# Low halves of 96 weight units by accumulating DMAs in a two-layer decoder trunk

## The chip, the cores and the metric

The kernel runs on one core of one Trainium2 chip. The metric is the device time of one execution in microseconds (us), lower is better. A profile gives, beside the time, the span from the first to the last instruction of the program on the core. The engines are TensorE (PE, with its weight loads PEld), VectorE (DVE), ScalarE (ACT), GpSimd (POOL) and SyncE (SP), which here issues every DMA.

## The reference

Two layers over a sequence of 512 positions with 1024 channels, all float32. Layer 0 mixes tokens with a gated DeltaNet, layer 1 with a Conformer convolution module; each layer then cross-attends into a fixed memory of 256 positions and applies a squared-ReLU MLP.

```python
for layer in range(DEPTH):                      # DEPTH = 2
    if layer % 2 == 0:
        h = h + gated_deltanet(rms_norm(h, ...), ...)
    else:
        h = h + conformer_conv(rms_norm(h, ...), w_pw1, ..., w_pw2, ...)
    h = h + memory_cross_attention(rms_norm(h, ...), rms_norm(mem, ...), w_q, w_kv, w_o)
    h = h + sq_relu_mlp(rms_norm(h, ...), w_up, w_down)
return rms_norm(h, final_norm)

def conformer_conv(h, w_pw1, b_pw1, w_dw, b_dw, ln_g, ln_b, w_pw2, b_pw2):
    u = h @ w_pw1 + b_pw1                       # 1024 -> 2048
    u = u[..., :D_MODEL] * jax.nn.sigmoid(u[..., D_MODEL:])
    c = causal_depthwise_conv(u, w_dw) + b_dw   # width 31
    c = jax.nn.silu(layer_norm(c, ln_g, ln_b))
    return c @ w_pw2 + b_pw2

def sq_relu_mlp(h, w_up, w_down):
    return jnp.square(jax.nn.relu(h @ w_up)) @ w_down   # 1024 -> 4096 -> 1024
```

## The kernel before

Every large product is made with three matmuls in the 32-bit format fp32r. An operand x is split into a rounded half xh and a rest xl = x - xh; a product is then xh·wh + xl·wh + xh·wl (`mm3`, lines 294 to 296; for K/V values and z lines 325 to 327; for the down projection lines 1104 to 1106). The activations are split where they are made, the weights while they stream through.

Weights come in units of 128 x 1024 floats (512 KB), 304 in all, in the order of the list `order`, which is written out by hand: projections of the DeltaNet, K and V of layer 0, output projection, attention and MLP of layer 0, then pw1 of the conformer with K and V of layer 1 behind it (`CONV_SEQ`), pw2, attention and MLP of layer 1. The MLP runs in four groups; a group is eight up units and fourteen down units. The down units are combined from quarters of the down weights on DVE first.

A unit passes through three steps.

- **Load.** `wload` (lines 206 to 217) has SP load the unit into a tile `raw`. The list `loads` gives the order and, for each load, the unit at which it falls due; an ordinary unit's load falls due four units ahead. `raw` has 3 buffers.
- **Split.** `wsplit` (lines 257 to 280) has ACT cast `raw` to the rounded half `wh` (line 273), and then DVE or POOL subtract: `wl = raw - wh` (line 273 calls the helper at line 75). POOL does this for the pw1 units that are not in `PW_DVE` (12 units) and for the first halves of K and V of layer 1 (8 units); DVE does it for all the others. `wh` and `wl` have 3 buffers each. Of the up and down units every fourth uses the tag `ex` instead (4 buffers, shared with some down loads).
- **Use.** `wnext` (lines 281 to 290) hands a unit to the matmuls. Before that it writes the splits of the next units: up to `NW_DN` = 4 counting its own in the MLP, `NW` = 3 elsewhere. A split can start only when the matmuls of an earlier unit have given its buffers free.

A unit for 512 columns is 24 matmuls of 512 columns; a down unit is 12. K and V work for 256 memory positions: a K unit is 24 matmuls of 256 columns, a V unit 12 of 512.

The waits between engines, and the final order on each engine's queue, are made by the framework out of the program order and the data each instruction touches; an engine's queue is then in order. In the conformer stage DVE and POOL also do the depthwise convolution: channel block 0 on POOL with multiplications on ACT (`pool_conv`, lines 1275 to 1290), blocks 1 to 4 on DVE in a PSUM tile (`dve_conv`, 1291 to 1307; line 1298 is its first tap on ACT, line 1304 its copy out), blocks 5 to 7 on PE (line 1335). The layer norm follows on DVE, its results are transposed on PE (line 1366), scaled on ACT (line 1368), and pw2 begins.

POOL's queue also has the sums of squares of the norms in the attention stages, the products of the attention probabilities with their reciprocal sums, and memsets.

Of the kernel before, what the change touches and what calls it, by code (L numbers as in the profile page):

```python
# [8 lines left out]
F32 = mybir.dt.float32  # L9
F32R = mybir.dt.float32r  # L10
AF = mybir.ActivationFunctionType
ALU = mybir.AluOpType
# [26 lines left out]
def tile_trunk(ctx, tc, xT, memT, prm_d, adt_d, bdw_d, tap_d, fin_d, w_ab, w_kq, w_v, w_z, w_dno, w_pw1, w_pw2,  # L39
               w_q, w_k, w_vv, w_o, w_up, w_dn, yT):  # L40
    nc = tc.nc
    pe, act, dve, pool = nc.tensor, nc.scalar, nc.vector, nc.gpsimd
# [3 lines left out]
    up = ctx.enter_context(tc.tile_pool(name="up", bufs=NSLOT))  # L46
# [12 lines left out]
    def big(s, tag, dt=F32):  # L59
        return wp.tile([P, 1024], dt, tag=tag, name=nm(s), bufs=NBIG[tag])  # L60
# [13 lines left out]
    def tt(e, o, a, b, op):  # L74
        return e.tensor_tensor(out=o, in0=a, in1=b, op=op)  # L75
# [65 lines left out]
    pool.memset(eps_ln, LN_EPS)  # L141


    order, loads = [], []

    def plan(key, src, n=2):
        for hf in range(n):
            unit(key, hf, src)

    def unit(key, hf, src):  # L150
        u = len(order)
        order.append((key, hf))
        loads.append((u - NRAW - 1, u, src[:, hf * 1024:(hf + 1) * 1024]))

    def plan_kv(layer, lo=0, hi=8):
        for i in range(lo, hi):
            if i < 4:
                plan(("K", layer, i), w_k[layer, i])
            else:
                plan(("V", layer, i - 4), w_vv[layer, i - 4])  # L160
# [20 lines left out]
    for kind, gq in DN_ORDER:  # L181
        for i in range(2):
            j = gq * 2 + i
# [7 lines left out]
    for kind, i in CONV_SEQ:  # L191
        if kind == "p":
            unit(("pw1", i // 2), i % 2, w_pw1[i // 2])
        elif i < 8:
            unit(("K", 1, i // 2), i % 2, w_k[1, i // 2])
        else:
            unit(("V", 1, i // 2 - 4), i % 2, w_vv[1, i // 2 - 4])
# [6 lines left out]
    ws = {"next": 0, "split": 0, "load": 1, "raw": {0: raw0}, "hl": {}}  # L204
# [14 lines left out]
    def wraw(key):  # L219
        while key not in ws["raw"]:  # L220
            wload()
        return ws["raw"][key]

    def parts(x, two):
        if isinstance(x, list):
            return x
        return [x[:, 0:512], x[:, 512:1024]] if two else [x]

    def dn_raw(layer, g, name, hf):

        def q(n):
            return wraw((layer, g, n, hf))

        def drop(n):
            return ws["raw"].pop((layer, g, n, hf))

        def sub(n, a, b):
            t = [q(k) for k in (n, a, b)]
            for v in zip(*(parts(x, any(isinstance(y, list) for y in t)) for x in t)):
                tt(dve, *v, ALU.subtract)  # L240
            return t[0]

        if name == "M1":
            return q("11"), lambda: sub("11", "12", "11")
        if name == "M5":
            return q("11"), lambda: sub("12", "22", "12")
        if name == "M6":
            return sub("11", "22", "11"), None
        if name == "M3":
            return drop("22"), None  # L250
        if name == "M7":
            return drop("12"), None
        if name == "M2":
            return q("21"), lambda: (sub("11", "21", "11"), drop("21"))
        return drop("11"), None

    def wsplit():
        u = ws["split"]
        ws["split"] += 1
        (kind, i, *j), hf = order[u]  # L260
        then = None
        if kind == "dn":
            raw, then = dn_raw(i, *j, hf)
        else:
            raw = wraw(u)
            del ws["raw"][u]
        extra = kind in ("up", "dn") and u % 4 == 3
        h = big("wh", "ex" if extra else "wh", F32R)
        lo = big("wl", "ex" if extra else "wl", F32R)
        gp = kind == "pw1" and (i, hf) not in PW_DVE or j and kind in "KV" and i == 1 and hf == 0  # L270
        two = isinstance(raw, list)
        for r, h_, l_ in zip(parts(raw, two), parts(h, two), parts(lo, two)):
            ins = [act.copy(h_, r), tt(pool if gp else dve, l_, r, h_.bitcast(F32), ALU.subtract)]  # L273
            if u < 4:
                for x in ins:
                    tc.keep_in_program_order(x)
        if then is not None:
            then()
        ws["hl"][u] = (h, lo)

    def wnext(key, hf):
        i = ws["next"]
        assert order[i] == (key, hf), (order[i], key, hf)
        while ws["load"] < len(loads) and loads[ws["load"]][0] <= i:
            wload()
        nw = NW_DN if key[0] in ("up", "dn") else NW
        while ws["split"] < min(i + (nw if i else 1), len(order)):
            wsplit()
        ws["next"] += 1
        return ws["hl"].pop(i)  # L290
# [550 lines left out]
    def mem_load():  # L841
        mem["m"] = []
        for j in range(4):
            m = slot(s="mem")
            nc.sync.dma_start(out=m, in_=memT[j])
            mem["m"].append(m)
# [32 lines left out]
    def mem_gain(layer, half):  # L879
        gn = f"xa_mem{layer}"  # L880
        if half == 0:
            mem["xs"] = []
        for j in (2 * half, 2 * half + 1):
            mh = slot(F32R, "mh")
            ml = slot(F32R, "ml")
            for i in range(2):
                ks = slice(i * 256, (i + 1) * 256)
                src = mem["m"][j][:, ks]
                g = pc(gn, 2 * j + i)
                act.activation(mh[:, ks], src, AF.Copy, scale=g)  # L890
                stt(ml[:, ks], src, g, mh[:, ks].bitcast(F32), ALU.mult, ALU.subtract)
                mem["xs"].append((mh[:, ks], ml[:, ks]))
        if half == 1:
            del mem["m"]

    KV = {}
# [314 lines left out]
    def taps(m):  # L1211

        TAPS[m] = []
        for i in range(9):
            t = slot(s="tap")
            nc.sync.dma_start(out=t, in_=tap_d[m - NTAP, i])
            TAPS[m].append(t)
# [189 lines left out]
    act.copy(ab3[:, :, 0:16], wab.rearrange("p (k x) -> p k x", k=KT))  # L1407
    tt(dve, ab3[:, :, 16:32], wab.rearrange("p (k x) -> p k x", k=KT), ab3[:, :, 0:16].bitcast(F32), ALU.subtract)
    wsplit()
    n0 = Norm("dn_norm", dve, False)  # L1410
    for t in range(KT):
# [37 lines left out]

    S.at(0, 0, squares, 0, SQ0)  # L1450
    S.at(0, 3, wsplit)
    S.at(0, 2, squares, SQ0, 8)
    S.at(T_STAT, 0, n0.stat)
# [24 lines left out]
    for gq in range(2):  # L1478
# [9 lines left out]
        for i in range(4):  # L1488
            h = 4 * gq + i
# [45 lines left out]
    h = []  # L1535
# [13 lines left out]
    h = xattn(0, n1, h, n2)  # L1549
    n3 = Norm("cv_norm", dve)  # L1550
    h = mlp(0, n2, h, n3, lambda i: mem_gain(1, i - 1) if i else (mem_load(), taps(NTAP)))
    n4 = Norm("xa_norm1")
    h = conformer(n3, h, n4)
    n5 = Norm("mlp_norm1")
    h = xattn(1, n4, h, n5)
# [12 lines left out]
DN_TAG = {("11", 0): "ex", ("11", 1): "ex", ("12", 0): "fs", ("12", 1): "fs", ("22", 0): "fs", ("22", 1): "cv",  # L1568
          ("21", 0): "cv", ("21", 1): "cv"}
DN_AHEAD = 3  # L1570
PW_DVE = ((0, 0), (0, 1), (1, 0), (1, 1))
NW_DN = 4
K_FIRST = (4, 5, 6, 7, 0, 1, 2, 3)
DN_ORDER = (("k", 0), ("q", 0), ("z", 0), ("v", 0), ("k", 1), ("q", 1), ("z", 1), ("v", 1))
# [121 lines left out]
```

## Time and profile before

| | |
|---|---|
| time, median of 3 runs | 1496.97 us (1496.8 to 1497.31) |
| profiled execution | 1496.75 us, its span 1495.0 us |
| granted TensorE clock | 0.997 |
| casts to `wh` on ACT (line 273) | 328 instructions, 320.6 us |
| subtractions to `wl` on DVE / POOL | 308, 353.7 us / 20, 49.0 us |
| matmuls of the up units | 3 x 512, 600 us |
| DMA | 154.63 MB, mean 103 GB/s, all program loads issued by SP |
| HBM read | 150.47 MB |

Some units of the down weights are split in two parts, so there are more casts than units. In the page's rows a group is named by line, engine, operation and out<-in; "busy" is the sum over its instructions and is followed by the mean of one in ns, then by the idle time of the engine just before them and what ended it. Times of a timeline are microseconds from the start of the span: start, duration, engine, line, operation. The time from issue to landing of a DMA is that from the issuing instruction to the signal that all of its data has arrived.

### The profile page before, as it was taken

The page shows a single profiled execution, that of the slowest core. Times are in us where ns is not written, and L with a number is a line of the kernel's source. Part 1 is how long each engine was busy: PE and PEld are TensorE (multiplying, and loading weights), DVE is VectorE, ACT ScalarE, POOL GpSimd, SP SyncE. Part 2 cuts the span into 40 slices and gives each one's busy share as a digit, 9 for nine tenths or more (in the row PEclk, how much of TensorE's full clock was granted, in tenths as well). Part 3 has the DMA queues.
Part 4 walks back from the last instruction along what each step waited for, and adds up shares of the span by engine and source line. Part 5 has one row for each costly group of instructions (what it writes and reads, how often), then busy time and mean ns, then how long its engine had stood idle before and what let it go on. Part 6 is the DMA issues. An engine that isn't in the chain of part 4 may idle for free.

```text
span 1495.0 us, 19728 instructions
## 1 busy us (share of the span) xinstructions
PE 1472.1 (98%) x7420; PEld 1241.4 (83%) x7420; DVE 1091.9 (73%) x1702; ACT 807.9 (54%) x1315; POOL 207.7 (14%) x221
## 2 busy tenths in 40 slices
PE   9999999999999999999999999989999999999998
PEld 7888888988888888888888889878888888888886
DVE  6898889866555585867769599975546585958677
ACT  6846655655444554536357654374435654545455
POOL 1321120102111000000000487212112000000000
PEclk9999999999999999999999999999999999999999
DMA  5221223542212314151542434543213224140501
GB/s 207 97 85 60 69 99 113 169 156 85 85 57 77 107 43 155 37 175 43 165 142 72 141 116 153 174 139 112 72 43 109 75 89 137 56 148 29 176 15 57
DMA packets 53231, 154.63 MB, mean 103 GB/s; under 512 B 6672, under 2 KB 8464, under 8 KB 53136
## 3 DMA queue, kind: packets, MB, share of 16 engines
q1 hardware_dynamic: 53136, 153.38, 31.3%
q8 instruction: 58, 0.95, 0.3%
q14 instruction: 37, 0.30, 0.1%
HBM read 150.47 MB, written 2.10 MB: 102 GB/s over the span
## 4 chain that ended last, share of the span: by engine, by line
PE 71%; DVE 7%; ACT 1%; SPq 1%; DMA 1%; issue 0%; ACTq 0%; DVEq 0%
PE up L294 8%; PE up L296 8%; PE up L295 8%; DVE ca L78 4%; PE dna L1104 4%; PE dna L1106 4%; PE dna L1105 4%; PE q L294 2%; PE xo L295 2%; PE q L295 2%; PE q L296 2%; PE xo L294 2%; PE xo L296 2%; PE dnc L1104 2%; PE dnc L1106 2%; PE dnc L1105 2%
## 5 line engine op out<-in xcount | busy, mean ns | idle before, releaser
L273 ACT CAST wh<-raw 128x1024 fp32r<-128x1024 f32 (+1 forms) x328 | 320.6, 987 | 441.2 <-PE up L295 99.2
L75 DVE TENSOR_TENSOR wl<-raw,wh 128x1024 fp32r<-128x1024 f32 (+1 forms) x308 | 353.7, 1159 | 209.2 <-ACT wh L273 207.0
L294 PE MATMUL up<-xh,wh 128*128 128x512 f32 x512 | 200.8, 392 | 0.0
L296 PE MATMUL up<-xh,wl 128*128 128x512 f32 x512 | 199.6, 390 | 0.0
L295 PE MATMUL up<-xl,wh 128*128 128x512 f32 x512 | 199.5, 390 | 0.0
L296 PEld LDWEIGHTS up<-xh,wl 128*128 128x128 f32 x512 | 96.2, 188 | 20.2
L295 PEld LDWEIGHTS up<-xl,wh 128*128 128x128 f32 x512 | 96.2, 188 | 19.5
L294 PEld LDWEIGHTS up<-xh,wh 128*128 128x128 f32 x512 | 96.2, 188 | 19.4
L78 DVE SCALAR_TENSOR_TENSOR ca<-x,prm,ca 128x512 f32<-128x512 f32 x120 | 87.9, 752 | 2.9 <-ACT ca L1298 1.3
L75 DVE TENSOR_TENSOR raw<-raw,raw 128x512 f32<-128x512 f32 (+1 forms) x96 | 81.1, 865 | 0.3
L294 PE MATMUL h<-xh,wh 128*128 128x512 f32 x192 | 77.5, 404 | 1.3 <-ACT xh L379 1.3
L295 PE MATMUL h<-xl,wh 128*128 128x512 f32 x192 | 75.4, 393 | 0.6 <-DVE xl L78 0.6
L296 PE MATMUL h<-xh,wl 128*128 128x512 f32 x192 | 75.6, 394 | 0.0
L75 POOL TENSOR_TENSOR wl<-raw,wh 128x1024 fp32r<-128x1024 f32 x20 | 49.0, 2455 | 72.2 <-ACT wh L273 55.5
L78 DVE SCALAR_TENSOR_TENSOR cva<-cv,prm,cva 128x512 f32<-128x512 f32 x60 | 49.4, 840 | 12.0 <-POOL cva L75 10.8
L75 POOL TENSOR_TENSOR sq<-sq,sq 128x512 f32<-128x512 f32 x24 | 38.0, 1585 | 136.4 <-ACT sq L386 103.7
L294 PE MATMUL pw<-xh,wh 128*128 128x512 f32 x128 | 50.3, 393 | 0.0
L294 PE MATMUL q<-xh,wh 128*128 128x512 f32 x128 | 50.2, 392 | 0.0
L295 PE MATMUL xo<-aol,wh 128*128 128x512 f32 x128 | 50.0, 391 | 0.0
L295 PE MATMUL q<-xl,wh 128*128 128x512 f32 x128 | 50.0, 390 | 0.0
L296 PE MATMUL pw<-xh,wl 128*128 128x512 f32 x128 | 49.9, 390 | 0.0
L296 PE MATMUL q<-xh,wl 128*128 128x512 f32 x128 | 49.9, 390 | 0.0
(403 smaller groups left out, 3616.7 us busy)
## 6 DMA issues: line engine op xcount, KB each, us to landing
raw<-w_up SPq DMA_DIRECT2D x64, 512.0 KB, 3.6
raw<-w_dn SPq DMA_DIRECT2D x40, 512.0 KB, 3.9
raw<-w_dn SPq DMA_DIRECT2D x48, 256.0 KB, 3.3
raw<-w_pw SPq DMA_DIRECT2D x24, 512.0 KB, 3.7
raw<-w_kq SPq DMA_DIRECT2D x16, 512.0 KB, 3.6
raw<-w_k SPq DMA_DIRECT2D x16, 512.0 KB, 4.5
raw<-w_vv SPq DMA_DIRECT2D x16, 512.0 KB, 3.6
raw<-w_q SPq DMA_DIRECT2D x16, 512.0 KB, 3.5
```

Of the source, the lines that this page charges most:

```text
L75: return e.tensor_tensor(out=o, in0=a, in1=b, op=op)
L78: dve.scalar_tensor_tensor(out=o, in0=a, scalar=s, in1=b, op0=op0, op1=op1)
L273: ins = [act.copy(h_, r), tt(pool if gp else dve, l_, r, h_.bitcast(F32), ALU.subtract)]
L294: pe.matmul(ps, wh, xh, start=first, stop=False)
L295: pe.matmul(ps, wh, xl, start=False, stop=False)
L296: pe.matmul(ps, wl, xh, start=False, stop=last)
L1104: pe.matmul(ps, ah[:, cs], w[hf][0][:, s_], start=fresh, stop=False, skip_group_check=more)
L1105: pe.matmul(ps, al[:, cs], w[hf][0][:, s_], start=False, stop=False, skip_group_check=more)
L1106: pe.matmul(ps, ah[:, cs], w[hf][1][:, s_], start=False, stop=end, skip_group_check=more)
```

## The change

For 96 units (the 64 up units, the 16 pw1 units, and the 16 units of K and V of layer 1) the subtraction is replaced. ACT makes, besides the rounded half, the negated rounded half in `wl`: `act.activation(lo, raw, AF.Copy, scale=-1.0)`, whose output type is fp32r, so it is rounded as `wh` is. Then a DMA issued on POOL's queue reads the same 512 KB of weights from HBM once more and adds them to `wl` where it lies: -wh + raw. The matmuls that read `wl` wait for that DMA. The dictionary `again` keeps, by unit, the piece of the weights in HBM. No affected unit is split on DVE or POOL any more, and `PW_DVE` goes; all other units are split as before, on DVE. The orders `order` and `loads`, the buffers and the lookahead stay.

```diff
-    order, loads = [], []
+    order, loads, again = [], [], {}
...
         loads.append((u - NRAW - 1, u, src[:, hf * 1024:(hf + 1) * 1024]))
+        if key[0] in ("up", "pw1") or key[0] in "KV" and key[1] == 1:
+            again[u] = loads[-1][2]
...
         h = big("wh", "ex" if extra else "wh", F32R)
         lo = big("wl", "ex" if extra else "wl", F32R)
-        gp = kind == "pw1" and (i, hf) not in PW_DVE or j and kind in "KV" and i == 1 and hf == 0
+        if u in again:
+            act.copy(h, raw)
+            act.activation(lo, raw, AF.Copy, scale=-1.0)
+            pool.dma_start(out=lo, in_=again[u], accum_op=ALU.add)
+            ws["hl"][u] = (h, lo)
+            return
         two = isinstance(raw, list)
         for r, h_, l_ in zip(parts(raw, two), parts(h, two), parts(lo, two)):
-            ins = [act.copy(h_, r), tt(pool if gp else dve, l_, r, h_.bitcast(F32), ALU.subtract)]
+            ins = [act.copy(h_, r), tt(dve, l_, r, h_.bitcast(F32), ALU.subtract)]
...
-PW_DVE = ((0, 0), (0, 1), (1, 0), (1, 1))
```

## The prediction

> **What bounds the kernel now.** I read the page's first part, then the chain that ended last, then the waits of TensorE (PE), and then the windows, to see in which stage any PE time is idle.
>
> ```profile
> PE 1472.1 (98%) x7420; PEld 1241.4 (83%) x7420; DVE 1091.9 (73%) x1702; ACT 807.9 (54%) x1315; POOL 207.7 (14%) x221
> PE 71%; DVE 7%; ACT 1%; SPq 1%; DMA 1%; issue 0%; ACTq 0%; DVEq 0%
> 579.00:623.00 44.00, 44.00 (x196) 36.45 (x195) 28.36 (x41) 23.83 (x36) 0.00 (x0) 1.00 0.22 72
> 826.00:923.00 97.00, 97.00 (x473) 81.76 (x472) 78.92 (x116) 56.52 (x104) 70.64 (x43) 1.00 0.37 117
> 923.00:998.00 75.00, 68.26 (x484) 62.17 (x483) 71.68 (x122) 33.69 (x52) 18.24 (x9) 1.00 0.58 193
> ```
>
> The three windows are an up stage, the pw1 stage and the K/V stage of the conformer (columns: stretch, length, busy PE, PEld, DVE, ACT, POOL with their counts, clock, DMA share, GB/s). PE is busy without a hole in the up and pw1 stages: less DVE work gains nothing there. Only the K/V stage has idle PE, 75.00 - 68.26 = 6.74 us, while DVE is busy 71.68 of 75. What PE waits for there:
>
> ```profile
> PE K L296 <- DVE wl L75: 1.5, 1, 1.5
> PE V L326 <- DVE wl L75: 1.3, 1, 1.3
> PE cvT L1319 <- ACT ca L1304: 1.8, 1, 1.8
> PE lnT L1366 <- ACT la L1368: 1.5, 1, 1.5
> 997.75 0.50 PE L294 MATMUL pw<-lsh,wh 128*128 128x512 f32 x1 [0.67 <-ACT la L1368]
> ```
>
> So the most that the change can win is these 6.7 us: two late low halves, a late convolution (its taps queue on DVE) and the layer norm behind it. The last row is where the stage ends, at the first matmul of pw2.
>
> **What goes and what comes.** 96 of 304 weight units change: 64 up, 16 pw1, 16 K/V of layer 1.
>
> ```profile
> L75 DVE TENSOR_TENSOR wl<-raw,wh 128x1024 fp32r<-128x1024 f32 x260 | 322.8, 1246 | 209.1 <-ACT wh L273 207.0
> L75 POOL TENSOR_TENSOR wl<-raw,wh 128x1024 fp32r<-128x1024 f32 x20 | 49.0, 2455 | 72.2 <-ACT wh L273 55.5 <-PE K L296 13.7 <-DVE ca L78 3.0
> L273 ACT CAST wh<-raw 128x1024 fp32r<-128x1024 f32 x280 | 293.1, 1051 | 412.6 <-PE up L295 99.2 <-issue 90.2 <-PE dna L1105 65.1
> L331 ACT CAST bh<-u 128x512 fp32r<-128x512 f32 x32 | 19.9, 622 | 1.1
> L1284 ACT ACTIVATE cvp<-xp,prm 128x512 f32<-128x512 f32 x7 | 5.0, 717 | 0.0
> L75 POOL TENSOR_TENSOR ca<-ca,cvp 128x512 f32<-128x512 f32 x30 | 40.5, 1349 | 11.6 <-ACT cvp L1286 6.2 <-ACT cvp L1284 3.9
> ```
>
> Gone: the 20 subtractions of POOL (49 us) and 76 of DVE (64 up, 4 pw1, 8 K/V), 76 x 1.246 = 95 us. All of it lies beside PE except in the K/V stage. Added on ACT: 96 negated copies. None is in the trace. The cast of the same tile takes 1.05 us; a scaled copy of half the width takes 0.72 us against 0.62 of a cast, which would make 1.2. I take 1.05, the same width: 101 us, with ACT at 23.83 of 44 in an up stage. That is hidden as a sum; what counts is that each one stands between its cast and its DMA. Added on POOL's queue: 96 DMA issues, each waiting for its ACT copy. Behind them on that queue stand the adds of convolution channel 0, the square sums of the norms and the x7 memsets; POOL loses 49 us of work, and I cost this queueing at nothing, and up to 1.35 us (one such add) ahead of an issue in pw1 at worst. Added traffic: 96 x 0.524 = 50 MB.
>
> **How long an accumulation takes.** No DMA of this trace is issued by POOL, and none accumulates, so it is bounded from the loads of the same 512 KB.
>
> ```profile
> q1 hardware_dynamic: 53136, 153.38, 31.3%
> raw<-w_up SPq DMA_DIRECT2D x64, 512.0 KB, 3.6
> 977.72 0.33 SPq L216 DMA_DIRECT2D raw<-w_pw  x1
> ```
>
> The queue's 153.38 MB took 31.3% of 1495.0 us, 468 us, so 512 KB takes 1.60 us of all 16 engines. Of the 3.6 us from issue to landing, 2.0 us are not data. An accumulation has two operands to fetch, the raw weights and the negated tile, so I take two passes, 3.2 us (bounds: one pass, 1.6, and three, 4.8). The issue lies between the 0.33 us of SP and the 2.455 us of the POOL subtraction; I take 1.2, nearer the first, since no data passes through POOL. Issue to landing is then 3.2 + 2.0 + 1.2 = 6.4 us, with ends 3.6 and 9.2. From the end of the cast to a usable low half it is 1.05 + 6.4 = 7.45 us, with ends 4.7 and 10.3.
>
> The Trainium skill ("Collectives: The Full Stack", Part 3, "Why ReduceScatter is half of AllGather") says that an add in the DMA path costs no time for its arithmetic but needs two reads, and gives 32.35 GB/s against 62.28 for the plain copy. No run here shows it yet. It speaks against this change: with one pass the landing would be 4.8 us and most of the loss below would vanish.
>
> **Against that, the lead of each unit.** I set the end of each cast against the first matmul that reads that unit's low half. Rows in pairs, cast and then matmul (twice with the matmul ahead of it, for the spacing); the last two are a load issue and the transposes behind the last V unit:
>
> ```profile
> 584.16 1.05 ACT L273 CAST wh<-raw 128x1024 fp32r<-128x1024 f32 x1 [4.38 <-PE up L295]
> 600.74 0.39 PE L295 MATMUL up<-xl,wh 128*128 128x512 f32 x1
> 600.97 0.39 PE L296 MATMUL up<-xh,wl 128*128 128x512 f32 x1
> ...
> 570.57 1.05 ACT L273 CAST wh<-raw 128x1024 fp32r<-128x1024 f32 x1 [1.62 <-PE dnb L1105]
> 579.21 0.39 PE L296 MATMUL up<-xh,wl 128*128 128x512 f32 x1
> ...
> 869.41 1.04 ACT L273 CAST wh<-raw 128x1024 fp32r<-128x1024 f32 x1
> 877.08 0.39 PE L296 MATMUL pw<-xh,wl 128*128 128x512 f32 x1
> ...
> 953.65 1.05 ACT L273 CAST wh<-raw 128x1024 fp32r<-128x1024 f32 x1 [7.35 <-DMA raw<-w_k]
> 957.56 0.28 PE L295 MATMUL K<-ml,wh 128*128 128x256 f32 x1
> 957.68 0.28 PE L296 MATMUL K<-mh,wl 128*128 128x256 f32 x1
> 978.10 1.04 ACT L273 CAST wh<-raw 128x1024 fp32r<-128x1024 f32 x1 [1.67 <-PE V L327]
> 986.00 0.39 PE L326 MATMUL V<-wl,mh 128*128 128x512 f32 x1
> 983.30 1.05 ACT L273 CAST wh<-raw 128x1024 fp32r<-128x1024 f32 x1 [0.64 <-PE V L327]
> 988.73 0.39 PE L326 MATMUL V<-wl,mh 128*128 128x512 f32 x1
> ...
> 946.06 0.86 SPq L216 DMA_DIRECT2D raw<-w_k  x2
> 993.88 1.03 PE L1366 MATMUL lnT<-ident,cy 128*128 128x128 f32 x8
> ```
>
> Up units inside a group have 600.97 - 585.21 = 15.76 us: covered even at 10.3. Cost 0.
>
> The first up unit of the later groups (six in all, three a layer) comes behind three short down units and has 579.21 - 571.62 = 7.59 us. At 7.45 it just fits; I put 1 us for all six, and 6 x (10.3 - 7.59) = 16 us at the upper end.
>
> In pw1 the cast runs late whenever ACT's queue stands behind DVE. The pair shown has 877.08 - 870.45 = 6.63 us and falls short by 0.8. Three more of the 16 units are alike (6.0 to 7.2 us), so some 3 us; with four DVE subtractions gone from this stage ACT should be less late, and I put 2.5 us.
>
> In K/V the unit takes PE only 24 x 0.12 or 12 x 0.227 = 2.8 us (0.12 and 0.227 are the spacing of the matmul starts), and there are three wl buffers: a buffer's round is cast, copy, accumulation and use, 1.05 + 1.05 + 6.4 + 2.8 = 11.3 us for three units, 3.8 us a unit against 2.8. Conv matmuls between them give the first six units time; ten units, K6 to V7, follow closely. K6 has 957.68 - 954.70 = 2.98 us, because its raw load was late: PE stands 4.5 us there. The V units have 6.86 (986.00 - 979.14), the last 4.38. Walked unit by unit with 6.4 us, V7 ends at about 999 instead of 993.88, where the transposes follow it. The DMA engines say more: ten units need 10 x (1.6 + 3.2) = 48 us of engine time, and from the first of their loads (946.06) that ends at 994 only with nothing else queued; but this stretch also loads pw2 and down weights, and its DMA share is already 0.58. Queueing one plain load ahead (1.6 us) gives a landing of 8 us, and the same walk ends at 1005. I take the middle, 1002, for V7. The waits of 6.74 us above are contained in these walks, since PE no longer reaches them early. The layer norm, freed on DVE, should be ready by then, so pw2 starts about 6 us after the 997.75 of before. Cost 6 us.
>
> **Sum:** 1 + 2.5 + 6 = 9.5 us on the profiled execution's 1496.75 us (span 1495.0 and 1.75 around it; the runs' median is 1496.97, 0.2 away): 1506 us.
>
> **Rivals.** *Faster.* If one pass of data suffices and the issue is short, the landing is under 4.8 us and the K/V leads hold except that of K6 (about 3 us). Of the 6.74 us then some 3.5 go: 1493 us. For it: DVE sheds the very work that PE waits for. Against it: the landing would have to be nearly that of a plain load. 0.12. *No change*, 1494 to 1500: a landing of 5 to 6 us, where stalls of K/V equal the waits that go. 0.18.
>
> *Late landing.* At the upper end, 9.2 us, nearly every unit with a lead under 10.3 is late: 16 us at the group starts, some 8 in pw1, 14 in K/V, 38 in all: 1535 us. It decides from a landing of about 7.5 us on, where the 7.59 of the group starts is passed by more than a microsecond each. Nothing in the trace excludes a slow issue on POOL. 0.10.
>
> *The DMA engines become the bound.* In an up unit of 24 x 0.227 = 5.44 us they must do 1.6 for the load and the accumulation; beyond 5.44 - 1.6 = 3.84 us for that, beside the down loads, the up stages stretch. At 5 us it is 64 x 1.16 = 74 us and some 30 in K/V: 1600 us. Against it: three passes of fetching are needed to get there. 0.10.
>
> *It doesn't do what it says:* the issues sit on POOL, so POOL is not empty of them, but its arithmetic is gone in any case; I give this no chance of its own.
>
> **How the numbers follow.** The forecast, 1500 to 1520 us, has 0.50. What a measurement can tell from no change is 0.2%, 3.0 us. Faster 0.12, same 0.18, slower 0.50 + 0.10 + 0.10 = 0.70. The range 1493 to 1540 leaves out the DMA-bound case (0.10), the tail of the late landing (0.03) and half of the faster case (0.06). Its lower end is the faster rival's time; its upper end is just past the late landing.
>
> **What would show it.** Right: ACT has 96 copies near 1.05 us; DVE is some 95 us and POOL's arithmetic 49 us shorter; HBM reads grow by 50 MB; a second DMA queue moves 50 MB; up windows stay full on PE; PE waits in K/V for DMA into wl, and a few times in pw1; pw2 starts near 1004. The rows of the accumulations give the issue-to-landing time that the sum takes as 6.4. Wrong: PE waits for wl inside up groups (DMA-bound), at all six group starts by 2 to 3 us (late landing), or nowhere (faster); or a time moved by something else than wl, such as the norms' adds behind issues on POOL.

## The result, and the profile after

| | before | after |
|---|---|---|
| time, median of 4 runs | 1497.14 us (1496.8 to 1498.04) | 1551.1 us (1547.13 to 1554.2) |
| span of the profiled execution | 1495.0 us | 1550.4 us |
| mean granted TensorE clock | 0.997 | 0.988 |
| the eight up stages of the two MLPs | 357.3 us | 381.3 us (+24.1) |
| pw1 | 96.7 us | 107.6 us (+10.8) |
| K/V of layer 1 | 74.5 us | 94.8 us (+20.3) |

The ratio is 1.0358, 95% interval 1.0333 to 1.0383: slower, as forecast, but by 54 us where 9.5 were worked out, and beyond the range. A stage's length, here and below, runs from the first matmul of the stage to the first of the next in the timeline. All other stages kept their length to 0.3 us.

The page of the changed kernel: the engines, the DMA queues (packets, megabytes, share of 16 engines over the span) and the chain.

```profile
PE 1488.0 (96%) x7420; PEld 1248.2 (81%) x7420; DVE 996.7 (64%) x1626; ACT 894.0 (58%) x1411; POOL 241.6 (16%) x297
...
q1 hardware_dynamic: 53136, 153.38, 30.0%
q0 software_dynamic: 13824, 50.34, 17.9%
...
PE 51%; issue 11%; DMA 9%; DVE 7%; ACT 2%; POOL 1%; SPq 0%; POOLq 0%; ACTq 0%
...
L275 POOL DMA_DIRECT2D wl<-w_up x64 | 56.5, 884 | 537.1 <-ACT wl L274 492.7
...
L274 ACT ACTIVATE wl<-raw 128x1024 fp32r<-128x1024 f32 x96 | 101.1, 1053 | 7.9 <-PE V L333 7.9
```

DVE lost the 95 us that were to go, the negated copy takes 1.053 us, an issue on POOL 0.884. The new queue q0 moved 50.34 MB in 17.9% of 1550.4 us, 277.5 us: 2.89 us of all 16 engines for each of 96 accumulations, against 1.60 for a plain load of the same size. In the chain, PE fell from 71% to 51%, and DMA rose from 1% to 9%. Where PE waits:

```profile
PE up L303 <- DMA wl<-w_up: 18.2, 9, 3.4
PE V L333 <- DMA wl<-w_vv: 7.4, 3, 3.4
PE K L303 <- DMA wl<-w_k: 7.4, 2, 5.4
PE pw L303 <- DMA wl<-w_pw: 7.2, 4, 2.8
PE cv L1342 <- DMA xg<-glu: 3.6, 2, 2.0
```

The columns are the total in us, the number and the longest. Four rows wait for accumulations, 40.2 us in 18 waits. The fifth is new too: 16 KB transfers that feed the convolution. The waits of before for DVE's low halves in this stage (1.5 + 1.3 us) are gone, as expected.

How long the DMAs take from issue to landing (median us, last column), and the windows of an up stage, pw1 and K/V (DMA share and GB/s are the last two columns):

```profile
raw<-w_up SPq DMA_DIRECT2D x64, 512.0 KB, 5.6
wl<-w_up POOLq DMA_DIRECT2D x64, 512.0 KB, 8.2
...
wl<-w_pw POOLq DMA_DIRECT2D x16, 512.0 KB, 7.7
...
wl<-w_k POOLq DMA_DIRECT2D x8, 512.0 KB, 8.1
wl<-w_vv POOLq DMA_DIRECT2D x8, 512.0 KB, 9.0
...
xg<-glu SPq DMA_DIRECT2D x48, 16.0 KB, 3.5
```

```profile
583.00:626.00 43.00, 41.72 (x184) 34.54 (x185) 19.97 (x34) 27.27 (x40) 5.21 (x6) 1.00 0.69 166
836.00:944.00 108.00, 100.56 (x473) 82.49 (x472) 80.30 (x122) 71.92 (x121) 54.17 (x47) 0.98 0.79 187
944.00:1038.00 94.00, 74.34 (x479) 66.94 (x477) 54.53 (x105) 45.15 (x65) 12.17 (x14) 0.91 0.90 234
```

A load of the up weights took 3.6 us before and takes 5.6 now; the small `xg` transfers took 1.8 and take 3.5. The DMA share rose from 0.22 to 0.69 in the up stage, from 0.37 to 0.79 in pw1, and from 0.58 to 0.90 in K/V. There is room left in up and next to none in K/V; the experiments come back to this difference.

The chain at the start of the second group of layer 0, in the timeline (start, duration):

```profile
573.91 1.05 ACT L273 CAST wh<-raw 128x1024 fp32r<-128x1024 f32 x1 [1.62 <-PE dnb L1112]
...
574.87 1.06 ACT L274 ACTIVATE wl<-raw 128x1024 fp32r<-128x1024 f32 x1
...
575.95 9.02 SPq L218 DMA_DIRECT2D raw<-w_up  x4
...
576.33 0.87 POOL L275 DMA_DIRECT2D wl<-w_up  x1 [52.74 <-ACT wl L274]
...
584.28 0.50 PE L303 MATMUL up<-xh,wl 128*128 128x512 f32 x1 [1.56 <-DMA wl<-w_up]
```

The negated copy ends at 575.93. It frees `raw`, so SP issues the next load at 575.95, and POOL the accumulation only at 576.33, behind it. The accumulation lands at 584.24 (7.91 us from its issue), and PE reads at 584.28. From the end of the cast (574.96) to usable it takes 9.3 us where the prediction has 7.45.

Two more parts of the loss are in no row of the waits. One of the stalls in pw1 is shown here, first in PE's timeline and then in windows of 3.2 to 3.4 us (the clock is the third column from the end):

```profile
892.09 0.39 PE L302 MATMUL pw<-xl,wh 128*128 128x512 f32 x1
895.25 0.50 PE L303 MATMUL pw<-xh,wl 128*128 128x512 f32 x1 [2.77 <-DMA wl<-w_pw]
895.58 0.39 PE L301 MATMUL pw<-xh,wh 128*128 128x512 f32 x1
```

```profile
892.00:895.20 3.20, 0.48 (x3) 0.06 (x1) 3.17 (x5) 2.67 (x6) 2.77 (x2) 1.00 1.00 250
...
896.60:900.00 3.40, 3.40 (x10) 2.63 (x9) 3.23 (x5) 2.77 (x6) 2.15 (x2) 0.50 0.25 54
900.00:903.40 3.40, 3.40 (x17) 2.77 (x16) 1.95 (x3) 1.38 (x2) 1.22 (x2) 1.00 0.85 200
```

A matmul starts every 0.227 us and lasts 0.39, so a wait of 2.77 us costs more than that: two starts lie 895.25 - 892.09 = 3.16 us apart instead of 0.227, and the next 0.33, so 3.03 us in all, 0.26 more than the row says. Then, from 896.6, the granted clock is 0.5 for 3.4 us, and 10 matmuls run in them where 17 run in the 3.4 us after. Apart from a stretch at the very start and one at the very end, which the trace of before has too, the trace has 27.3 us at half clock, one stretch of 6.83 us and six of 3.41, each beside a stall; PE was still standing in 4.0 of them. In the other 23.3 the starts of 512-column matmuls are 0.427 us apart instead of 0.227, so about 11 us are lost.

The sum: 40.2 us of waits for accumulations, 3.6 for the convolution's transfers, 20 x 0.26 = 5.2 around these waits, 11 of half clock, less some 5 us of waits of before that went, make 55 of the 55.4 us of span.

### The profile page after: what moved, and what is told of

The parts are those of the page before. It is cut to its first block, busy times and chain, and to the rows that moved or that the text cites. A ratio compares the mean times of both kernels' runs of the same rounds, so it can differ in the third digit from the quotient of the medians.

```text
span 1550.4 us, 19948 instructions
## 1 busy us (share of the span) xinstructions
PE 1488.0 (96%) x7420; PEld 1248.2 (81%) x7420; DVE 996.7 (64%) x1626; ACT 894.0 (58%) x1411; POOL 241.6 (16%) x297
## 3 DMA queue, kind: packets, MB, share of 16 engines
q0 software_dynamic: 13824, 50.34, 17.9%
## 4 chain that ended last, share of the span: by engine, by line
PE 51%; issue 11%; DMA 9%; DVE 7%; ACT 2%; POOL 1%; SPq 0%; POOLq 0%; ACTq 0%
PE up L303 7%; PE up L301 7%; PE up L302 7%; DMA wl<-w_up 5%; DVE wl L75 3%; DMA wl<-w_pw 2%; PE q L301 2%; PE q L303 2%; PE q L302 2%; PE xo L302 2%; PE xo L301 2%; PE xo L303 2%; PE pw L303 2%; PE pw L301 2%; PE pw L302 2%
## 5 line engine op out<-in xcount | busy, mean ns | idle before, releaser
L280 ACT CAST wh<-raw 128x1024 fp32r<-128x1024 f32 (+1 forms) x232 | 219.9, 962 | 283.1 <-issue 60.0
L75 DVE TENSOR_TENSOR wl<-raw,wh 128x1024 fp32r<-128x1024 f32 (+1 forms) x232 | 256.0, 1116 | 93.7 <-ACT wh L280 92.0
L273 ACT CAST wh<-raw 128x1024 fp32r<-128x1024 f32 x96 | 100.6, 1050 | 157.9 <-PE up L302 72.9
L275 POOL DMA_DIRECT2D wl<-w_up x64 | 56.5, 884 | 537.1 <-ACT wl L274 492.7
L274 ACT ACTIVATE wl<-raw 128x1024 fp32r<-128x1024 f32 x96 | 101.1, 1053 | 7.9 <-PE V L333 7.9
L78 DVE SCALAR_TENSOR_TENSOR y<-dna,rb,y 128x512 f32<-128x512 f32 x64 | 46.1, 745 | 49.1 <-PE dna L1113 49.1
L75 DVE TENSOR_TENSOR al<-u,al 128x256 fp32r<-128x256 f32 x32 | 13.5, 421 | 89.4 <-ACT al L1073 89.4
L75 DVE TENSOR_TENSOR s<-u,u 128x256 f32<-128x256 f32 x32 | 13.6, 425 | 75.3 <-ACT u L1069 75.3
L78 DVE SCALAR_TENSOR_TENSOR cva<-cv,prm,cva 128x512 f32<-128x512 f32 x60 | 49.4, 840 | 12.0 <-POOL cva L75 10.8
```

What stands on the lines that cost most here:

```text
L78: dve.scalar_tensor_tensor(out=o, in0=a, scalar=s, in1=b, op0=op0, op1=op1)
L273: act.copy(h, raw)
L274: act.activation(lo, raw, AF.Copy, scale=-1.0)
L275: pool.dma_start(out=lo, in_=again[u], accum_op=ALU.add)
L280: ins = [act.copy(h_, r), tt(dve, l_, r, h_.bitcast(F32), ALU.subtract)]
```

## The experiments

Two theories, after the result. *Lead:* an accumulation is usable about 9.3 us after its cast, and PE waits wherever the cast has less lead than that. *Engines:* 96 transfers of 2.89 us fill the DMA engines, and everything is late by their number. Lost time against the kernel before, by stage, from the profiled executions (us):

| | up | pw1 | K/V | ratio of times, 95% interval |
|---|---|---|---|---|
| the change | 24.1 | 10.8 | 20.3 | 1.0358, 1.0333 to 1.0383 |
| E1 up units only | 21.1 | 0 | 0 | 1.015, 1.0134 to 1.0165 |
| E2 pw1, K, V only | 0 | 11.9 | 19.4 | 1.0235, 1.022 to 1.025 |
| E3 late up units only | 0 | 0 | 0.1 | 1.0, 0.9991 to 1.0009 |
| E4 copy ahead of cast | 19.1 | 14.3 | 19.8 | 1.0346, 1.0332 to 1.036 |
| E5 no addition | 1.0 | 6.6 | 5.6 | 1.0084, 1.0067 to 1.0101 |
| E6 four units ahead | 20.0 | 5.3 | 16.4 | 1.025, 1.0223 to 1.0278 |
| E7 low products last | 0 | 4.0 | 9.4 | 1.009, 1.0075 to 1.0105 |
| E8 before, low products last | 0 | 0 | -1.8 | 0.9989, 0.998 to 0.9998 |
| E9 half the columns | 1.3 | 4.8 | 7.3 | 1.0096, 1.0081 to 1.011 |
| E10 E6 and E7 together | 0 | 9.4 | 15.1 | 1.0184, 1.0168 to 1.02 |
| E11 eight units, low last | 0 | 0 | 2.7 | 1.0025, 1.0015 to 1.0034 |
| E12 up units only, low last | 0 | 0 | 1.6 | 0.9994, 0.9985 to 1.0003 |

(In E7, E8 and E10 to E12 the first up stage starts 0.7 to 1.7 us later than before, but in E1, with the old order of the products, it also starts 1.0 us later. The columns don't contain this.)

### E1, E2, E3: parts of the change

```diff
-        if key[0] in ("up", "pw1") or key[0] in "KV" and key[1] == 1:
+        if key[0] == "up":                                              # E1
+        if key[0] == "pw1" or key[0] in "KV" and key[1] == 1:           # E2
+        if key[0] == "up" and 2 * (key[2] % 4) + hf >= 3:               # E3
```

All other units are split as in the kernel before, on DVE and POOL. E1:

> Only the 64 up units get accumulating DMAs; pw1, K and V are split as before. Theory (lead): time is lost only where a low half lands later than its unit's matmuls want it, and by the half-clock windows that the longer stalls bring. In the changed kernel the up stages lost 24 us by the starts of the stages (15.5 at the six group starts behind down units, 8.6 at the two behind the attention) and the conformer 31. Expected 1497 + 24 = 1521 us (1515 to 1527), with PE waiting for DMA into wl about 18 us in all. Rival (traffic): the second reading of the weights costs by its bytes, 64 of 96 units, so 36 us: 1533.

E2:

> Only the 16 pw1 units and the 16 K/V units of layer 1 get accumulating DMAs; the up units are split as before. Lead theory: 11 us in pw1 and 20 in K/V as in the changed kernel, 1528 us (1522 to 1534). Traffic rival: 32 of 96 units, 18 us: 1515.

E3:

> Accumulating DMAs only for the fourth to eighth up unit of each group (40 of 96), whose low halves were wanted 15 us or more after the cast before. Lead theory: landing 9.3 us after the cast's end is early enough for all of them, no stall, and nothing gained as PE was full in these stages: 1497 us within 2. Traffic rival: 40 of 96 units, 22 us: 1519.

E1 took 1519.22 us, E2 1532.92, E3 1497.69. The losses of E1 and E2 are those of the change in the same stages to within 3 us, and they nearly add up: the two parts hardly disturb each other. The waits of E1, then of E2:

```profile
PE up L304 <- DMA wl<-w_up: 15.1, 9, 2.2
```

```profile
PE V L334 <- DMA wl<-w_vv: 7.7, 4, 3.5
PE pw L304 <- DMA wl<-w_pw: 7.6, 4, 2.8
PE K L304 <- DMA wl<-w_k: 7.0, 2, 5.7
PE cv L1343 <- DMA xg<-glu: 3.2, 2, 2.2
```

E3 keeps 40 of the 64 accumulations of up, those of the fourth to eighth unit of each group. The queue and the landings of E3's page:

```profile
q0 software_dynamic: 5760, 20.97, 8.0%
...
wl<-w_up POOLq DMA_DIRECT2D x40, 512.0 KB, 7.6
```

They land about as late as in the change (median 7.6 us; 8.2 there over all 64), and PE waits for none. In the up stages the theory of lead holds: the traffic of these 40 costs nothing, and the loss belongs to the first three units of the groups.

### E4: the copy ahead of the cast

```diff
-            act.copy(h, raw)
             act.activation(lo, raw, AF.Copy, scale=-1.0)
             pool.dma_start(out=lo, in_=again[u], accum_op=ALU.add)
+            act.copy(h, raw)
```

> All 96 units as in the change, but ACT makes the negated copy first, then the DMA is issued, and the cast to the high half comes after. Lead theory: every accumulation starts 1.05 us earlier, the 22 stalls shrink by about as much each and some half-clock windows go: about 1551 - 22 - 7 = 1522 us (1515 to 1535). Rival (the 16 DMA engines are the bound): landing is set by what the engines have to move, an earlier issue changes nothing: 1548 to 1552.

1549.02 us, which reads like the rival. The timeline of ACT at the same group start says why it is none:

```profile
573.88 1.05 ACT L276 CAST wh<-raw 128x1024 fp32r<-128x1024 f32 x1 [1.62 <-PE dnb L1113]
574.83 1.06 ACT L274 ACTIVATE wl<-raw 128x1024 fp32r<-128x1024 f32 x1
```

Line 276, the cast, still runs ahead of line 274, and so it does in the first unit of all eight groups, whose accumulation is then issued no earlier. A likely reason, not shown, is that the framework orders the queue by when buffers come free, and that of `wh` is read for the last time before that of `wl`. This run decides nothing.

### E5: the same transfers without the addition

```diff
-            pool.dma_start(out=lo, in_=again[u], accum_op=ALU.add)
+            pool.dma_start(out=lo, in_=again[u])
```

> All 96 transfers on GpSimd's queue as in the changed kernel, at the same places and behind the same negated copies, but they overwrite the low tile instead of adding to it. What is left out: the addition, so the low tiles hold the raw weights. Theory A (the second operand that an accumulation reads makes it land late): 16 engines' time per transfer falls from 2.9 us to about 1.6, the landing from 8.2 us to about 6, and some 20 stalls shrink by about 2 us each, half-clock windows with them: 1505 to 1520. Theory B (the landing is late because these transfers queue beside the weight loads and behind a fixed part, the addition itself being nothing): landing 7.5 or more, 1540 to 1550.

1511.6 us. The queue, the landing, and the waits that are left:

```profile
q0 software_dynamic: 13824, 50.34, 10.2%
...
wl<-w_up POOLq DMA_DIRECT2D x64, 512.0 KB, 5.4
```

```profile
PE K L304 <- DMA wl<-w_k: 4.0, 2, 3.6
PE pw L304 <- DMA wl<-w_pw: 3.9, 4, 2.2
PE V L334 <- DMA wl<-w_vv: 3.4, 4, 1.2
...
PE up L304 <- DMA wl<-w_up: 0.7, 1, 0.7
```

10.2% of 1507.8 us is 153.8 us, 1.60 a transfer: without the addition it costs the engines what a plain load does, and it lands 2.8 us sooner. Theory A. The addition nearly doubles the engine time (2.89 / 1.60 = 1.8) for the same bytes from HBM, and some 40 of the change's 54 us go with it.

### E9: half the columns

E5 leaves open whether the addition costs engine time or has a delay of its own.

```diff
-            pool.dma_start(out=lo, in_=again[u], accum_op=ALU.add)
+            pool.dma_start(out=lo[:, :512], in_=again[u][:, :512], accum_op=ALU.add)
```

> The changed kernel with every accumulation cut to the first 512 of its 1024 columns; the addition to the other half of each low tile is left out. Count, issue, place and the second operand stay, the bytes halve. The run without the addition had 1.60 us of 16 engines per transfer and landed after 5.4 us against 2.89 and 8.2. Theory A (it is the work in the DMA engines): 1.45 us of 16 engines per transfer, landing 5 to 5.8 us, time like that run's, 1505 to 1517. Theory B (an accumulation has a delay of its own, reading the tile back, that doesn't hang on its size): landing 7 us or more, 1535 to 1550.

1511.35 us:

```profile
q0 software_dynamic: 13824, 25.17, 10.1%
...
wl<-w_up POOLq DMA_DIRECT2D x64, 256.0 KB, 5.8
```

1.59 us of 16 engines per transfer (1.45 was expected), landing 5.8 us, and a time like E5's, with the addition kept. So it is mostly the work in the engines, and not a delay of the addition.

### E6, E7, E8, E10: more lead

E6 gives pw1, K and V a second set of tiles and a fourth unit ahead:

```diff
-        extra = kind in ("up", "dn") and u % 4 == 3
+        extra = (kind in ("up", "dn") or u in again) and u % 4 == 3
...
-        nw = NW_DN if key[0] in ("up", "dn") else NW
+        nw = NW_DN if key[0] in ("up", "dn") or i in again else NW
```

> All 96 accumulations, but pw1 and the conformer's K and V units get the longer lead of the up units inside a group: every fourth unit in a second set of tiles, and four units ahead instead of three. Lead theory (about 9.3 us from the cast's end to usable against the lead of each unit): a unit of pw1 gains 3.6 us or more of lead and one of K or V 3.6; the 31 us that pw1, K and V lost go mostly, the 24 of the up groups' starts stay: 1520 to 1527. Rival (the engines or GpSimd's queue are full in these stages, so that a longer lead only lets more transfers wait): 1542 to 1550.

E7 leaves the issues where they are and needs them later; V is changed in the same way. E8 is the kernel before with this order.

```diff
-            mm3(ps, wk(w, k), xs[k], k == 0, k == KT - 1)
+            wh = wk(w, k)[0]
+            pe.matmul(ps, wh, xs[k][0], start=k == 0, stop=False)
+            pe.matmul(ps, wh, xs[k][1], start=False, stop=False)
+        for k in range(k0, k1):
+            pe.matmul(ps, wk(w, k)[1], xs[k][0], start=False, stop=k == KT - 1)
```

> All 96 accumulations, but the products with the low weights of a unit (8 of its 24 matmuls, 16 of 48 in V) come after its other products, so that the low half is needed about 3.6 us later in an up or pw1 unit and about 1.9 us later in K. Lead theory: the stalls of up (18.2 us in nine of at most 3.4 us) and of pw1 (7.2) are covered, the half-clock windows there with them, and of K and V's 15 us in five stalls about 5 to 8 stay: 1503 to 1515. Rival (the transfers are late by their number, so what is late once stays late): 1535 to 1550.

> The kernel before with the same order of the products (low weights last in each unit), as control for the run with this order: 1494 to 1498. Any order of the products costs nothing by itself if this holds; were it 1500 or more, part of what the order does in the changed kernel would be due to the order alone.

E7 took 1512.42 us, E8 1496.11, E6 1538.62. The waits of E7:

```profile
PE V L345 <- DMA wl<-w_vv: 5.6, 7, 1.8
PE cv L1353 <- DMA xg<-glu: 3.0, 2, 2.0
PE K L316 <- DMA wl<-w_k: 2.7, 2, 2.0
...
PE pw L316 <- DMA wl<-w_pw: 2.0, 2, 1.7
...
PE pw L304 <- DMA wl<-w_pw: 1.0, 1, 1.0
```

No row of up is left: 3.6 us of lead cover all eight group starts, with all accumulations still there, landing no sooner (8.7 us). The theory of lead got this stage and the total right. In pw1 and K/V 13.4 of 31.1 us stay.

E6 contradicts the theory. With a longer lead it should have won back most of those 31 us, and won 9.4 (21.7 of 31.1 stay). Its time lies between the two expectations and meets neither. So both remedies were put together:

> All 96 accumulations in full, with both remedies: low-half products last in each unit, and four units ahead in pw1, K and V. If only the lead of each unit counts, next to nothing is left of the loss: 1496 to 1502. Rival (in pw1 and K/V the DMA engines are full: in the changed kernel 0.79 of 107.5 us and 0.89 of 94.8 us, 169 us in all, where the kernel before took 171 us for the two stages, and 84 us against 74.5 in K/V alone): K/V stays at 82 us or more however long the lead, 1504 to 1512, with a DMA share of 0.9 or more in K/V.

1525.12 us, slower than E7 alone. The windows of K/V in E7 and then in E10, and the waits of E10:

```profile
928.00:1011.80 83.80, 71.28 (x481) 63.24 (x479) 55.39 (x106) 45.40 (x65) 12.21 (x14) 0.98 0.93 258
...
933.70:1023.30 89.60, 73.64 (x482) 65.48 (x481) 55.23 (x107) 43.60 (x67) 16.92 (x18) 0.92 0.89 249
```

```profile
PE V L345 <- DMA wl<-w_vv: 7.0, 5, 5.0
PE lnT L1384 <- DVE cy L84: 4.7, 1, 4.7
PE cv L1353 <- DMA xg<-glu: 4.3, 4, 1.7
```

In K/V and pw1 lead alone is not enough. The transfers of the K/V stage took 0.93 x 83.8 = 78 us of the engines in E7 and 0.89 x 89.6 = 80 us in E10, where the whole stage lasted 74.5 us before: some 3.5 of the 9.4 us that E7 still loses there are the engines' time alone, as long as these transfers fall into this stage. In this the rival is right in kind. It isn't right in size, since it allowed 1504 to 1512.

The engines' time doesn't say why E10 is slower than E7, with the same 96 transfers. In these two stages E10 loses 11 us more, and most of that is in two waits, 5.0 us for the accumulation of a V unit and 4.7 for the layer norm on DVE, and in 17.1 us at half clock against 3.4. Later plain loads don't explain it alone: those of `w_pw` land after 6.5 us (E7: 5.3), but those of `w_k` and `w_vv` after 3.9 and 5.3 (E7: 4.4 and 6.2). Why E10 has these two waits is not settled.

The prediction offers a third reading of K/V, its round of the three `wl` buffers. With the landings measured, 8.1 and 9.0 us, the round is 13.0 to 13.9 us, 4.3 to 4.6 us a unit against 2.8, and ten units would lose 15 to 18 us by it alone. The further tiles of E6 and E10 should then have won back most of it, and K/V still lost 16.4 and 15.1 us. This speaks against buffers as the main cause, but the further tiles are shared with down loads, so it doesn't exclude them.

### E11, E12: what is left of the change

```diff
+SAFE = [(("pw1", 1), 0), (("pw1", 7), 1)] + [(("K", 1, k), hf) for k in range(3) for hf in range(2)]
-        if key[0] in ("up", "pw1") or key[0] in "KV" and key[1] == 1:
+        if (key, hf) in SAFE:                                           # E11
+        if key[0] == "up":                                              # E12
```

Both have the order of E7.

> Only eight accumulations, all in the conformer and with a lead of 13 us or more in the kernel before (two of pw1, K's first six units), the other 88 low halves subtracted as before, low-half products last in each unit. By the lead theory none is waited for; what DVE sheds (6 subtractions in K, one or two of pw1) may remove part of the waits for DVE in K/V: 1492 to 1497, at or below the 1496.1 of the order alone. Rival (any accumulation in K/V costs, since its engines are loaded to 0.58 and raw loads come later): 1498 to 1504.

> Only the 64 up units accumulate (1519.2 us with the old order of the products), now with the low-half products last in each unit; pw1, K and V as in the kernel before. Lead theory: in these stages the DMA engines have room (the forty late units of each group cost nothing), so 3.6 us more lead covers the starts of all eight groups, and 64 accumulations cost nothing: 1495 to 1498, like the order alone (1496.1), with no wait of TensorE for an accumulation in up. Rival (what the longer landings take comes back as late loads or waits elsewhere): 1502 or more.

E11 took 1501.57 us, E12 1496.73. The first wait of PE in E11:

```profile
PE cv L1353 <- DMA xg<-glu: 3.5, 2, 3.3
```

E11's rival holds, by another way than it named. No unit waits for its accumulation, but PE waits for the convolution's 16 KB transfers: they land after 4.1 us instead of 1.8, PE stands 3.3 us, and a half-clock stretch of 6.83 us follows. E12 confirms E3 and E7: 64 accumulations, two thirds of the change, cost nothing once each has its lead (E1, the same without it, lost 21 us); the 1.6 us of its K/V are one wait of the convolution for ACT in the profiled execution, and its median shows nothing of them. It gains nothing either, since DVE wasn't late in up. Against the kernel before, E8, the order alone, has the lowest ratio, 0.9989 (0.998 to 0.9998), without any accumulation; its interval overlaps that of E12.

## Why the prediction was wrong

**Right:** the sign; the copy, 1.05 us; the issue on POOL, 1.2 assumed and 0.40 + 0.88 measured from the copy's end to the issue's; two passes of data, 3.2 assumed and 2.89 measured; units inside a group at nothing, from the fourth on (E3); the places: group starts, four units in pw1, the end of K, and V. The sign was not luck: most of PE's new waits for `wl` lie where the prediction had found short leads.

**The step that failed** is the landing, 3.2 + 2.0 + 1.2 = 6.4 us; it measured 8.2 (up), 7.7 (pw1), 8.1 (K) and 9.0 (V). Each piece was sound, but they were added as if the accumulation were alone. One term is missing: the copy that releases the accumulation also releases a load, which SP issues 0.38 us sooner on the same 16 engines, 1.60 us. With it the sum at the group start shown is 0.87 + 2.0 + 1.60 + 2.89 = 7.4 us, of 7.91. The last three accumulations of the last group have no weight load beside them; they landed after 5.5, 5.3 and 5.8 us, and the sum without the load is 5.8. The prediction had the term, but only in one of its two walks for K/V. The trace of before had this load, one behind each unit:

```profile
572.90 8.92 SPq L216 DMA_DIRECT2D raw<-w_up  x4
```

There it follows the subtraction, on the tile that this frees. The Trainium skill ("DMA: Bandwidth & Descriptors", "Issuing engines are not separate DMA queues") says that transfers issued by different engines share the 16 DMA engines and interleave; the trace agrees (loads of up 3.6 to 5.6 us).

*Group starts, 1 us.* The landing of 6.4 "just fits" a lead of 7.59: a term that hangs on 0.14 us was taken at its middle. At 9.3 each of the six is late by 1.6 us or more: 15.5 us for six. The first groups after the attentions had no term and lost 8.6 together: PE waited there for the second unit in both and for the third in one, units inside a group, which the prediction put at nothing.

*pw1, 2.5 us,* measured 10.8, four late units as foreseen, each 1.4 to 2.8 us late.

*K/V, 6 us,* measured 20.3. The walk with a landing of 8 us, about what was measured, ended only 3 us later than the 1002 that was taken, so the landing alone doesn't make the 20.3. Two steps failed beside it. The first six units were given time, and the longest wait of the stage, 5.4 us, is for the sixth K unit. Its load stood on SP's queue behind 16 of the convolution's transfers, whose issues took from 949.58 to 967.73; four of them waited until an earlier transfer of the convolution's taps had landed, 6.7 us in all. The load was issued at 967.73, its accumulation landed at 984.7, and PE went on. The other step is the DMA engines' time: 48 us for ten units fitted "only with nothing else queued", and of all that else was queued one load was counted. A count over the whole stages would have decided it: 0.37 x 97 + 0.58 x 75 = 79 us of transfers were there, and 32 accumulations at the 3.2 us assumed are 102 more, 181 us where the two stages last 172. With 2.89 it is 172; measured in the windows after: 0.79 x 108 + 0.90 x 94 = 170 us. For up the same count gives 0.22 x 44 + 8 x 2.89 = 33 of 44 us, room to spare. The rival that the DMA engines become the bound was argued for up, where it is wrong (E3, E12), at 1600 us, and hardly for K/V, where the engines' time is at least a part of the loss (E7, E10).

*Half clock and the pipeline around a wait: no terms,* about 11 and 5 us.

**The rivals.** *Late landing,* from 7.5 us on, is what happened in up and in part of the rest, with a chance of 0.10 only, and priced at 38 us for a landing of 9.2 instead of 55 us for one of about 8.2: it had neither the engines' count nor the half clock. The range's upper end came from that price. The rule of two reads (the Trainium skill, "Collectives: The Full Stack", Part 3), which the page gives for rings of several cores, has a ratio of 62.28 / 32.35 = 1.93; E5 against the change gives 1.8, so the trace nearly agrees.

## What to carry to other kernels

Before work moves from a compute engine to DMAs, count for each stage the engine time that is there (DMA share times length) and the new transfers times theirs (an accumulation counted 1.8 loads): where the sum nears the length of the stage, lead wins back only a part (13.4 of 31.1 us stayed with E7, 24.5 with E10). Where there is room, set issue, landing *and the transfers released by the same instruction* against the lead of the least favoured unit, and make lead by consuming the late operand last (E12). A change that wins only when an engine with slack gets more slack is worth nothing, however cheap.

## What was not expected of the hardware

**The clock.** Over the 14 profiled executions here, in the stages from the first K/V on, all 22 stalls of PE of 2.66 us or more ran into a stretch of 3.41 or 6.83 us at a granted clock of 0.5; between 1.9 and 2.6 us it went both ways. No single stall below 1.9 us did, but in E2 two of 0.94 and 0.67 us, with four transposes between them, were followed by a stretch at 1028.9, so the length of one stall is not the whole rule. The stall of 2.77 us shown above, with its half-clock stretch, cost about 4.6. The Trainium skill ("TensorE: Matmul & The Clock Gate", Part 1) describes a free-running window of 3413 ns and half rate after at least one idle window. The traces agree on the length of 3.413 us and on the half rate; that 1.92 us can do, and 2.66 always did, is shorter than a window, and here the measurement decides.

**The accumulating DMA.** It takes 2.89 us of 16 engines for 512 KB against 1.60 without the addition (E5) and 1.59 for 256 KB with it (E9).

**Small transfers beside large ones.** The 16 KB transfers of the convolution landed after 3.5 us instead of 1.8, and one late one of them cost E11 more than its eight accumulations were worth.
